# Regrouping the sample rows' narrow matmuls and splitting the opening of the channel mixer in a two-layer decoder step

## The chip, the cores and the metric

The kernel runs on one core of a Trainium2 chip. The metric is device time in microseconds of one execution. Before the change it takes 2732.52 us (median of 3 runs, 2725.46 to 2732.99).

## The reference

Two layers work on 1024 prompt rows and 32 sample rows (8 sequences of 4 new tokens, each with 1024 cached keys in pages), width 1024. Cut to what the change touches:

```python
for l in range(2):
    # sample rows: score all 1028 keys with 8 small index heads, take the best 256, attend
    dots = einsum('bqhd,bsd->bqhs', qi, ki_all) * 64 ** -0.5
    sc   = einsum('bqhs,bqh->bqs', relu(dots), wi)
    _, idx = top_k(where(causal, sc, -inf), 256)
    o = softmax(q @ kg.T * 64 ** -0.5) @ vg          # on the 256 keys taken
    x = layer_norm(ALPHA * x + concat(conv_mixer, o, chunk_mixer) @ w_o)
    h = causal_dwconv3(x @ w_up)                      # 1024 -> 2 x 2816
    x = layer_norm(ALPHA * x + (silu(g) * u) @ w_down)   # g, u = halves of h
```

All inputs and outputs are float32.

## The kernel before

**Stages of a layer.** The input projection with the index, the threshold search, the key and value work, the attention of eight prompt blocks with the sample attention beside blocks 2 to 4, the output projection and norm, then the channel mixer in two parts: 22 chunks of the up projection (`up_chunk`), and the down projection in three teams of 4, 3 and 3 groups (L1919). Large products run as three float32r matmuls (high by high, high by low, low by high), so each operand is split into two parts: ScalarE makes the high part, VectorE or GpSimd subtracts to get the low part (`split`, L618).

**Order.** Every instruction is recorded first (`record`, L317) with a cost from a small model (`cost`, L371) and a priority, which is the program order plus a shift, less a multiple of the length of work behind it. `flush` (L409) then simulates the engines: on each engine the ready instruction of lowest priority goes next, and instructions are issued in that simulated order. Engines take them in that order on the chip. Writers of one PSUM tile on TensorE follow each other in program order (`pe_last`).

**Narrow matmuls.** Three stages of the sample rows use products with 64 or 32 output rows, each put in another part of the same PSUM tile. They are float32 and appear as two records each.
- `index_sample` (L982): per layer 2 x 2 times, two gathered cache tiles (p2 = 0, 1) are transposed, copied to `kgT`, and each half multiplied into 64 rows of one PSUM tile (L1027).
- `scores` (L1346): per layer 8 rounds; four cache tiles are transposed, copied in two copies of two tiles to `kt`, and four products into 32 rows each follow (L1366). `values` (L1405) multiplies, for 8 chunks of keys, four gathered value tiles into 32 rows each.
- `down_sample` (L1874): for each of 10 groups two weight tiles (i = 0, 1), each loaded by a DMA, are multiplied in two halves of columns into 32 rows each of the tile `sm`. The weight tiles lie in the buffers raw, hiA, loA, hiB, loB. The loop over a team's groups is at L1925.

**Opening of the channel mixer.** The up projection is a 2 x 2 block product with seven products, A11.B11, A12.B21, S2.T2, S1.T1, S4.B22, S3.T3, A22.T4, in this order, each 24 matmuls of 128 rows by 268 or 270 columns (`up_product`, L1705). A and S are weights or sums of weights, made by `up_weights` (L1667); B and T are transposed activations or sums of them. `fill` (L1812) makes the activations once per layer, within chunk 0 and ahead of its first product: norms of tiles 6 and 7 (`CARRY`), then for each of the nine tiles a spill to memory, transposes, copies and splits (`put_block`, L1781). Tiles 0 to 3 give B11 and B21; tile t from 4 to 7, with tile t - 4, gives B22, T1 to T4, whose sums GpSimd or VectorE makes. When tile 3 is done, `put_edges` (L1796) writes the first columns of all seven operands.

```python
for t in CARRY:
    layer_norm_direct(fd, y[t], 128, *rows_, D)
for t in (8, 3, 4, 0, 1, 5, 2, 6, 7):
```

Of the kernel before, what the change touches and what calls it, by code (L numbers as in the profile page):

```python
# [19 lines left out]
D = 1024  # L20
# [24 lines left out]
X_OPS = ("B11", "B21", "T2", "T1", "B22", "T3", "T4")  # L45
BIG = float(2.0 ** 100)
MINI, MAXI = -2147483648, 0x7FFFFFFF
NEG = -3.0e38
# [155 lines left out]
class Schedule:  # L204
# [4 lines left out]
    def __init__(self, tc):  # L209
        self.tc, self.nc = tc, tc.nc  # L210
        self.ops = []
        self.hist = {}
        self.free = {e: 0.0 for e in self.LAT}
        self.dma_free = 0.0
        self.base = 0
        self.shift = 0
        self.slack = 0.0
        self.crit = 0.0
        self.tags = {}
        self.slot_of = {}  # L220
        self.fin = {}
        self.held = {}
        self.gone = set()
        self.dead = set()
        self.also = ()
        self.slot_no = {}
        self.stacks = {}
        self.side_of = {}
        self.extents = {}
        self.pe_last = {}  # L230

    def engine(self, name, real):
# [84 lines left out]
    def record(self, eng, fn, method, args, kwargs):  # L317
# [14 lines left out]
        op["slack"] = self.slack  # L332
        op["cost"], op["xfer"] = self.cost(eng, method, kwargs, aps_w, aps_r)
        for write, aps in ((False, aps_r), (True, aps_w)):
            for a in aps:
# [73 lines left out]
    def flush(self):  # L409
# [80 lines left out]
        while done < n:  # L490
# [22 lines left out]
            o = ops[i]  # L513
            o["start"] = start
            end = start + o["cost"]
            self.free[e] = end
# [29 lines left out]
def trunk(ctx: ExitStack, tc: tile.TileContext, A):  # L546
# [293 lines left out]
    for l in range(DEPTH):  # L840
# [141 lines left out]
        def index_sample():  # L982
# [16 lines left out]
            for j in range(2):  # L999
# [17 lines left out]
                for q in range(2):  # L1017
                    kgi = T(wk, [128, 8, 2, 64], F32, "kgi", 1)
                    kT_ = T(wk, [128, 8, 128], F32, "kgT", 1)
                    for p2, kg in enumerate(kgs):  # L1020
# [5 lines left out]
                        ACT.activation(kT_[:, 4 * p2:4 * p2 + 4, :], tp2, AF.Copy)  # L1026
                    for p2 in range(2):  # L1027
                        PE.matmul(dsp[q][64 * p2:64 * p2 + 64], qbd[:, 2 * j + p2, :], kT_[:, 4 * p2:4 * p2 + 4, :],
# [312 lines left out]
        def attend_sample(ts):  # L1341
# [4 lines left out]
            def scores(j):  # L1346
# [10 lines left out]
                for h in range(4):  # L1357
                    kt = T(ts, [128, 4, 2, 128], F32, "kt", KTB)
                    for i in range(2):
# [5 lines left out]
                        copy(kt[:, 2 * i:2 * i + 2], tp2, KT_DVE[(2 * h + i) % len(KT_DVE)])  # L1365
                    for b4 in range(4):  # L1366
                        PE.matmul(ss[h // 2][32 * b4:32 * b4 + 32, 256 * (h % 2):256 * (h % 2) + 256],
# [37 lines left out]
            def values(j):  # L1405
# [6 lines left out]
                for c in range(8):  # L1412
                    for b4, vg in enumerate(vgs):
                        PE.matmul(O[32 * b4:32 * b4 + 32], PT[:, c, 32 * b4:32 * b4 + 32], vg[:, c, :],
# [251 lines left out]

        def up_weights(c):  # L1667
            raws = [T(wp, [128, 1024], F32, "raw", RAWB) if c % 2 == 0 else stride_tile(4 + i)[:, :1024] for i in range(2)]
# [7 lines left out]

            w = slots(("A11", "A12", "S2", "S1"))
            split(*w["A11"], a11)
            split(*w["A12"], a12)
            if c == 0:  # L1680
                w.update(slots(("S4", "S3", "A22")))
# [17 lines left out]
            if c:  # L1699
                split(*w["A22"], a22)  # L1700
            return w

# [26 lines left out]

        def up_chunk(c, between=None):  # L1730
            w = up_weights(c)
            ncf = T(fd, [128, 2, 18], F32, "ncf", 2)
            stf = T(fd, [128, 2, 8, 2], F32, "stf", 2)
            SP.dma_start(stf, A["state_ffn"][l, :, 2 * c:2 * c + 2])
            if between is not None:
                between()
            rg, ru, zg, zu = (stride_tile(t).rearrange("p (h n) -> p h n", h=2) for t in (0, 1, 2, 3 + 4 * (c % 2)))
# [3 lines left out]
            for cut, ps in up_product(ga, w, "A12", "B21", True):  # L1741
                V.tensor_add(rg[:, 0, cut], rg[:, 0, cut], ps)
            for cut, ps in up_product(al, w, "S2", "T2", False):
                ACT.activation(rg[:, 1, cut], ps, AF.Copy)
# [50 lines left out]

        def put_edges():  # L1796
            e11, e21, e12, e22 = edge[:, 0, 0:4], edge[:, 0, 4:8], edge[:, 1, 0:4], edge[:, 1, 4:8]
# [4 lines left out]

            for n, e in (("B11", e11), ("B21", e21), ("B22", e22)):
                put(n, e)
            V.tensor_sub(e12, e22, e12)
# [5 lines left out]

        def fill():  # L1812
            PL.memset(edge, 0.0)
            for t in CARRY:
                layer_norm_direct(fd, y[t], 128, *rows_, D)
            for t in (8, 3, 4, 0, 1, 5, 2, 6, 7):
                r0, n = row(t)
# [8 lines left out]
                elif t < 4:  # L1826
# [4 lines left out]
                    if t == 3:  # L1831
                        put_edges()
                if t >= 4 and t < 8:
# [17 lines left out]
        for c in range(NFF):  # L1851
            zu = up_chunk(c, None if c else fill)
            if c % 2:
# [20 lines left out]
        def down_sample(ps, xs_, raws, begun, last):  # L1874
            for i, x_ in enumerate(xs_):
                for h in range(2):
                    q = 32 * (2 * i + h)
                    PE.matmul(ps[q:q + 32], x_, raws[i][:, 512 * h:512 * h + 512], start=q not in begun,
                              stop=last, skip_group_check=True)
# [39 lines left out]
        for team in TEAMS:  # L1919
# [4 lines left out]
            raws = {g: down_raws(g) for g in gs}  # L1924
            for g in gs:  # L1925
                down_sample(smp, [xf[:, 2 * g + i] for i in range(2)], raws[g], begun, g == NPAIR - 2)
            sch.shift = 0
# [193 lines left out]
```

## Time and profile before

| | |
|---|---|
| median of 3 runs | 2732.52 us |
| profiled execution, its own time | 2729.01 us |
| its span, first to last instruction | 2727.1 us |
| mean granted TensorE clock | 0.979 |
| bytes read from and written to HBM | 193.95 and 64.04 MB |

Busy time is the time in which an engine had at least one instruction running. In a list of instructions the first two numbers are start and duration in microseconds, x is how many were merged in a row, and a bracket shows the idle time before and what ended it. Matmuls are pipelined, so they last longer than the distance to the next. All instructions carry the line 540, at which the planner issues them; they are told apart by their tiles. PSUM tiles of several uses share the name w, and operands of the mixer lie in buffers named a and q.

### The profile page before, as it was taken

How to read it: one execution, taken by the hardware profiler on the slowest of the kernel's cores; microseconds unless marked ns; L12 is line 12 of the kernel's file. 1: busy time of each engine (PE TensorE's matmuls, PEld its weight loads, DVE VectorE, ACT ScalarE, POOL GpSimd, SP SyncE). 2: the span in 40 equal slices, each digit the busy share in tenths (PEclk: the TensorE clock that was granted, in tenths of full speed). 3: DMA queues.
4: the chain of work that ended last, by engine and by line, in shares of the span. 5: the costliest groups of instructions: out<-in, count | busy, mean ns of one | idle time of the engine just before them, and what ended most of it. 6: DMA issues, size and time to landing. Idle time of an engine off the chain costs nothing.

```text
span 2727.1 us, 47611 instructions
## 1 busy us (share of the span) xinstructions
PE 2574.7 (94%) x17217; PEld 2301.5 (84%) x17220; DVE 2179.5 (80%) x4788; ACT 1427.4 (52%) x2796; POOL 1062.6 (39%) x1399
## 2 busy tenths in 40 slices
PE   8989989997999999999999999889889999999996
PEld 7889976787999999777887898668789999997775
DVE  6788888878778777877778988878778777788776
ACT  3678537655444444434446775475544444544433
POOL 5244164563222222543362423635632222225433
PEclk9999999998999999999999999999989999999998
DMA  5021123302223222643231212131123322236432
GB/s 168 17 70 60 55 86 117 103 34 70 95 92 104 98 87 95 241 166 110 79 100 32 65 62 93 60 120 60 56 64 103 102 92 95 87 116 220 167 107 81
DMA packets 120339, 261.07 MB, mean 96 GB/s; under 512 B 29224, under 2 KB 39144, under 8 KB 120104
## 3 DMA queue, kind: packets, MB, share of 16 engines
q1 hardware_dynamic: 114216, 237.07, 26.4%
q0 software_dynamic: 5888, 20.97, 2.4%
q8 instruction: 135, 2.21, 0.3%
q14 instruction: 100, 0.82, 0.1%
HBM read 193.95 MB, written 64.04 MB: 95 GB/s over the span
## 4 chain that ended last, share of the span: by engine, by line
PE 76%; DVE 14%; POOL 2%; ACT 2%; issue 2%; DMA 2%; SPq 1%; POOLq 0%; DVEq 0%; ACTq 0%
PE w L540 70%; DVE y L540 3%; PE wo L540 3%; DVE loA L540 1%; PE o L540 1%; DVE cand L540 1%; DVE gt L540 1%; DVE P L540 1%; PE sm L540 1%; DVE pl L540 1%; DVE q L540 1%; POOL raw L540 1%; PE ss L540 1%; DVE sc L540 1%; SPq L540 1%
## 5 line engine op out<-in xcount | busy, mean ns | idle before, releaser
L540 PE MATMUL w<-q,hiB 128*128 128x268 f32 (+1 forms) x2112 | 402.8, 289 | 2.9 <-DVE y L540 2.3
L540 PE MATMUL w<-q 128*128 128x512 f32 x1680 | 396.2, 395 | 5.3 <-DVE q L540 5.3
L540 PE MATMUL w<-q,hiA 128*128 128x268 f32 (+1 forms) x2112 | 398.2, 288 | 0.0
L540 PEld LDWEIGHTS w<-q 128*128 128x128 f32 x1680 | 313.6, 188 | 98.6 <-issue 20.1
L540 PEld LDWEIGHTS w<-q,hiB 128*128 128x128 f32 x2112 | 331.7, 189 | 9.0 <-DVE y L540 9.0
L540 PEld LDWEIGHTS w<-q,hiA 128*128 128x128 f32 x2112 | 331.0, 189 | 0.0
L540 ACT ACTIVATE y<-w 128x268 f32<-128x268 f32 (+1 forms) x356 | 140.2, 394 | 354.5 <-PE w L540 345.6
L540 PE MATMUL w<-q,loB 128*128 128x268 f32 (+1 forms) x1056 | 304.4, 288 | 0.0
L540 PE MATMUL w<-q,loA 128*128 128x268 f32 (+1 forms) x1056 | 302.9, 287 | 0.0
L540 DVE SCALAR_TENSOR_TENSOR y<-y,cvf,y 128x1075 f32<-128x1075 f32 (+1 forms) x176 | 236.5, 1344 | 46.8 <-ACT y L540 45.8
L540 DVE TENSOR_TENSOR y<-y,w 128x512 f32<-128x512 f32 (+2 forms) x400 | 201.4, 514 | 71.4 <-PE w L540 68.9
L540 ACT ACTIVATE eq<-sc,cand 128x640 bf16<-128x640 f32 (+2 forms) x192 | 192.6, 1003 | 32.7 <-DVE cand L540 28.8
L540 ACT ACTIVATE q<-a 128x512 fp32r<-128x512 f32 x148 | 90.2, 625 | 220.2 <-PE w L540 160.6
L540 PEld LDWEIGHTS w<-q,loA 128*128 128x128 f32 x1056 | 199.6, 189 | 0.0
L540 PEld LDWEIGHTS w<-q,loB 128*128 128x128 f32 x1056 | 199.2, 189 | 0.0
L540 DVE TENSOR_SCALAR_CACHE_REDUCE gt<-sc,cand 128x384 bf16<-128x384 f32 (+4 forms) x204 | 161.7, 792 | 0.9
L540 POOL COPY ncf<-y 128x16 f32<-128x16 f32 (+1 forms) x176 | 108.7, 625 | 111.2 <-DVE y L540 111.2
L540 DVE TENSOR_TENSOR q<-a,q 128x512 fp32r<-128x512 f32 x148 | 124.1, 851 | 28.3 <-ACT q L540 26.0
L540 PE MATMUL w<-a,hiA 128*128 128x270 f32 (+1 forms) x704 | 135.3, 288 | 0.0
L540 POOL TENSOR_SCALAR P<-P,rc 128x128 f32<-128x128 f32 (+7 forms) x104 | 86.0, 837 | 106.5 <-DVE rc L540 79.5
L540 ACT ACTIVATE ph<-w 128x512 fp32r<-128x512 f32 (+1 forms) x160 | 84.3, 554 | 82.4 <-PE w L540 74.1
L540 ACT ACTIVATE y<-y,cvf 128x1076 f32<-128x1076 f32 x88 | 104.8, 1191 | 38.7 <-DVE y L540 34.6
(423 smaller groups left out, 7295.4 us busy)
## 6 DMA issues: line engine op xcount, KB each, us to landing
fspill<-y SPq DMA_DIRECT2D x148, 256.0 KB
a<-fspill SPq DMA_DIRECT2D x148, 256.0 KB
raw<-w_up SPq DMA_DIRECT2D x44, 512.0 KB
y<-w_up SPq DMA_DIRECT2D x44, 512.0 KB
raw<-w_nat SPq DMA_DIRECT2D x20, 512.0 KB
raw<-w_tr SPq DMA_DIRECT2D x16, 512.0 KB
raw<-w_o SPq DMA_DIRECT2D x16, 512.0 KB
yspill<-y SPq DMA_DIRECT2D x16, 512.0 KB
```

The costliest lines, as they stand in the source:

```text
L540: o["fn"](*o["args"], **o["kwargs"])
```

## The change

It reverses the order within the rounds of the index, the scores, the values and the down samples; runs the down samples' groups of the first team as 1, 0, 3, 2 and those of the others last to first; splits `up_weights` into steps and `fill` into two parts, so that tiles 8, 3, 0, 1, 2 and then the first two products come before the other weights, the norms of tiles 6 and 7 and tiles 4 to 7; and adds 0.1 us to the planner's cost of a TensorE instruction whose shape differs from the one before.

```diff
+SHAPE_COST = 0.1
...
+        if eng == "PE":
+            k, m = int(aps_r[0].shape[0]), int(np.prod([int(v) for v in aps_r[0].shape[1:]]))
+            op["shape"] = tuple(32 if v <= 32 else 64 if v <= 64 and aps_r[1].dtype == F32 else 128 for v in (k, m))
...
+            if e == "PE" and o["shape"] != self.shape:
+                self.shape = o["shape"]
+                o["cost"] += SHAPE_COST
             end = start + o["cost"]
...
-                    for p2 in range(2):
+                    for p2 in (1, 0):
                         PE.matmul(dsp[q][64 * p2:64 * p2 + 64], qbd[:, 2 * j + p2, :], kT_[:, 4 * p2:4 * p2 + 4, :],
...
-                    for b4 in range(4):
+                    for b4 in (3, 2, 1, 0):
                         PE.matmul(ss[h // 2][32 * b4:32 * b4 + 32, 256 * (h % 2):256 * (h % 2) + 256],
...
-                    for b4, vg in enumerate(vgs):
+                    for b4, vg in reversed(list(enumerate(vgs))):
                         PE.matmul(O[32 * b4:32 * b4 + 32], PT[:, c, 32 * b4:32 * b4 + 32], vg[:, c, :],
...
-        def up_weights(c):
+        def up_weights(c, w):
...
-            w = slots(("A11", "A12", "S2", "S1"))
+            w.update(slots(("A11", "A12", "S2", "S1")))
             split(*w["A11"], a11)
             split(*w["A12"], a12)
+            yield
             if c == 0:
...
-            return w
+            yield
...
-        def up_chunk(c, between=None):
-            w = up_weights(c)
+        def up_chunk(c):
+            w = {}
+            begin = up_weights(c, w)
+            next(begin)
+            if c == 0:
+                fill((8, 3, 0, 1, 2))
+            else:
+                next(begin)
...
-            if between is not None:
-                between()
...
             for cut, ps in up_product(ga, w, "A12", "B21", True):
                 V.tensor_add(rg[:, 0, cut], rg[:, 0, cut], ps)
+            if c == 0:
+                next(begin)
+                for u in CARRY:
+                    layer_norm_direct(fd, y[u], 128, *rows_, D)
+                put_edges(False)
+                fill((4, 5, 6, 7))
             for cut, ps in up_product(al, w, "S2", "T2", False):
...
-        def put_edges():
+        def put_edges(first):
...
-            for n, e in (("B11", e11), ("B21", e21), ("B22", e22)):
-                put(n, e)
+            if first:
+                for n, e in (("B11", e11), ("B21", e21)):
+                    put(n, e)
+                return
+            put("B22", e22)
...
-        def fill():
-            PL.memset(edge, 0.0)
-            for t in CARRY:
-                layer_norm_direct(fd, y[t], 128, *rows_, D)
-            for t in (8, 3, 4, 0, 1, 5, 2, 6, 7):
+        PL.memset(edge, 0.0)
+
+        def fill(tiles):
+            for t in tiles:
...
-                        put_edges()
+                        put_edges(True)
...
-            zu = up_chunk(c, None if c else fill)
+            zu = up_chunk(c)
...
-            for i, x_ in enumerate(xs_):
+            for i in (1, 0):
...
-                    PE.matmul(ps[q:q + 32], x_, raws[i][:, 512 * h:512 * h + 512], start=q not in begun,
+                    PE.matmul(ps[q:q + 32], xs_[i], raws[i][:, 512 * h:512 * h + 512], start=q not in begun,
...
-            for g in gs:
-                down_sample(smp, [xf[:, 2 * g + i] for i in range(2)], raws[g], begun, g == NPAIR - 2)
+            for g in (1, 0, 3, 2) if first else gs[::-1]:
+                down_sample(smp, [xf[:, 2 * g + i] for i in range(2)], raws[g], begun, g0 == NPAIR - 1 and g == gs[0])
```

## Rows read from the trace of the kernel before

**Rows 1.** The page: busy time of each engine, and the chain that ended last.
```profile
PE 2574.7 (94%) x17217; PEld 2301.5 (84%) x17220; DVE 2179.5 (80%) x4788; ACT 1427.4 (52%) x2796; POOL 1062.6 (39%) x1399
...
PE 76%; DVE 14%; POOL 2%; ACT 2%; issue 2%; DMA 2%; SPq 1%; POOLq 0%; DVEq 0%; ACTq 0%
```

**Rows 2.** Busy time by stretch: length, engines, granted clock, DMA share, GB/s.
```profile
84.00:137.00 53.00, 53.00 (x350) 42.45 (x349) 42.89 (x95) 34.10 (x77) 13.65 (x29) 1.00 0.08 21
1440.00:1485.00 45.00, 45.00 (x295) 35.04 (x293) 36.45 (x78) 30.02 (x70) 11.57 (x21) 1.00 0.09 24
426.00:481.00 55.00, 50.06 (x399) 36.42 (x400) 43.38 (x131) 43.20 (x98) 19.35 (x23) 1.00 0.35 118
1776.00:1835.00 59.00, 53.90 (x411) 39.60 (x411) 42.66 (x127) 41.05 (x91) 18.08 (x21) 0.93 0.27 89
610.00:641.20 31.20, 15.89 (x106) 12.61 (x105) 29.76 (x55) 17.50 (x40) 15.50 (x12) 0.73 0.20 68
1965.80:1998.40 32.60, 16.33 (x106) 13.88 (x106) 31.16 (x56) 17.25 (x40) 15.24 (x13) 0.69 0.29 98
1107.00:1127.00 20.00, 17.66 (x81) 9.70 (x80) 16.86 (x14) 9.82 (x16) 16.80 (x13) 1.00 0.85 309
```

**Rows 3.** TensorE's timeline: two key products of the index, one chunk-mixer round.
```profile
89.13 1.07 PE L540 MATMUL w<-kgT,qbd 128*64 128x512 f32 x2
90.13 0.41 PE L540 MATMUL w<-kiTs,qall 64*128 64x32 f32 x2
...
1467.25 1.07 PE L540 MATMUL w<-kgT,qbd 128*64 128x512 f32 x2
...
38.82 0.66 PE L540 MATMUL w<-wmT,nat 128*64 128x128 f32 x8
39.41 0.42 PE L540 MATMUL w<-hiA,xlo 128*128 128x328 f32 x1
```

**Rows 4.** The chain in order of time, sample attention: start, us, what.
```profile
464.45 0.56 PE ss L540 x4
...
470.87 0.57 PE ss L540 x8
```

**Rows 5.** TensorE's waits: us in total, times, the longest.
```profile
PE ss L540 <- ACT kt L540: 1.5, 2, 1.3
...
PE sm L540 <- DMA raw<-w_down: 1.0, 1, 1.0
```

**Rows 6.** TensorE's timeline: value rounds of the first layer.
```profile
452.68 1.95 PE L540 MATMUL w<-kg,kt 128*32 128x128 f32 x64
...
488.71 1.06 PE L540 MATMUL w<-kg,kt 128*32 128x128 f32 x26
```

**Rows 7.** The chain in order of time, down projection of the first layer.
```profile
1137.07 1.84 PE sm L540 x12
...
1155.40 0.98 PE sm L540 x4
...
1166.54 6.38 DMA raw<-w_down
...
1181.27 0.99 PE sm L540 x8
```

**Rows 8.** TensorE's timeline: opening of the channel mixer, first layer.
```profile
624.74 1.09 PE L540 MATMUL w<-ident,q 128*128 128x128 f32 x4 [10.58 <-DVE ln_ve L540]
...
641.12 0.49 PE L540 MATMUL w<-a,hiA 128*128 128x268 f32 x2
...
648.94 0.28 PE L540 MATMUL w<-q,hiA 128*128 128x268 f32 x1
```

**Rows 9.** Timelines of ScalarE and VectorE in the same opening.
```profile
629.83 0.29 ACT L540 ACTIVATE q<-edge 128x104 fp32r<-128x104 f32 x1 [11.90 <-DVE edge L540]
...
627.80 1.28 DVE L540 SCALAR_TENSOR_TENSOR y<-y,ln_rs,q 128x1024 f32<-128x1024 f32 x1 [1.08 <-POOL ln_rs L540]
...
647.35 0.68 DVE L540 TENSOR_TENSOR q<-w,q 128x512 fp32r<-128x512 f32 x1
```

More of the change, by code (lines that the diff above doesn't have):

```diff
@@ L230, in __init__ @@
         self.pe_last = {}
+        self.shape = None
     def engine(self, name, real):
```

## The prediction

> **What bounds the kernel now.** I read the page first: TensorE is busy 94% of the span and holds 76% of the chain that ended last; VectorE is 80% busy and holds 14% [rows 1]. So time that goes from TensorE counts wherever TensorE has no gaps, and the busy time by stretch says where that is [rows 2]. The index of the sample rows (84 to 137 us, and 1440 to 1485 in the second layer) has none: 53.00 of 53.00 us. The sample attention (426 to 481, 1776 to 1835) is 91% full. The opening of the channel mixer (610 to 641, 1966 to 1998) is the opposite: TensorE works 15.9 of 31.2 us, VectorE 29.8, so VectorE sets its pace. The opening of the down products (1107 to 1127) lies between: TensorE 17.7 of 20, VectorE 16.9, DMA at 0.85.
>
> Then the timeline, for the narrow products. In all three sample stages a product fills only 32 or 64 of the 128 array columns and its neighbours take the others. One 64-wide key product of the index holds TensorE from 89.13 to 90.13, 1.00 us; there are 8 such, all alone, per layer, and the last of the second layer at 1467.25 is as long [rows 3]. The 64-wide products of the chunk mixer, two in each half, are issued together: four of 128 columns, 512 in all, take 0.59 us (38.82 to 39.41), where one key product of 512 columns takes 1.00 [rows 3]. So halves run side by side. In the scores two products (four records) take 0.56 us, and four products (eight records) 0.57 [rows 4]. In the down samples one half-round (four records) takes 0.98, a whole one (eight) 0.99, and twelve records 1.84 [rows 7]. A half-round that stands alone costs as much as a whole one: that is what the regrouping acts on.
>
> **The change part by part.** The durations are of the profiled execution, 2729.0 us; the median of the three runs lies 3.5 us above it.
>
> *Index rounds.* The second half now leads, so the first, ready long before, can follow at once. 8 lone products per layer become 4 pairs: 8 x 1.00 = **8.0 us** over both layers, all on a TensorE without a gap. From below 5, if some pairs are split. Nothing new waits: the tile of both halves was freed by the second before, too.
>
> *Score rounds.* In each layer 7 of 8 rounds stand as two halves of 0.56 and one as a whole. Regrouped that is 14 x 0.56 = 7.8 us. In the first layer 11 of the 14 halves' records lie on the chain of waits (rows such as the first of [rows 4]); 11/14 of 7.8 is **6.1**. Bounds 3 and 7.8: the stretch has 9% of gaps that a shorter TensorE does not close.
>
> *Value rounds.* The first group's 64 records go in one piece, 1.95 us; the second group's are cut into pieces, the largest 26 [rows 6]. Its pieces have 10, 26, 20, 6 and 2 records, and all four operands had landed after the first four products, so it was the plan's priorities that cut, not an operand. Reversing the operands does not mend that. I take **0.5**; from above 3 (both second groups gathered), below 0.
>
> *Down samples.* From 1127 on TensorE is full. There each layer spends now 12 records (1.84), four lone halves before 1190 (0.98 each), two wholes (0.99), two lone halves late in the second team: 9.7 us. After: a two-round piece of the first team 1.84, and three rounds for each of the other teams, 0.99 + 2 x 0.85 = 2.69 (0.85 is what a further round adds, 1.84 - 0.99); 7.2 in all. That is 2.5 per layer. One wait for a weight load, 1.0 us in the first layer [rows 5], goes with it, since the leader is placed at the last load. Together **6.0**. Ahead of 1127 another 3.9 us per layer of rounds would go, but there they fill a TensorE that waits for operands (VectorE 16.9 of 20 us busy [rows 2]): I count 0, from above 7.8. VectorE and DMA are the cover of these rounds; where the operands came earlier they would count. What is moved is only the matmul order; the loads themselves keep theirs on SP's queue. The GpSimd subtractions that overwrite the raw rows must wait for the gathered rounds, but those of a team come two products, 17 us or more, after its start.
>
> *Mixer opening.* The two products A11.B11 and A12.B21 take 6 us and now may start when tiles 0 to 3 stand. But they already overlap the tail: they start at 641.12, while the third product S2.T2 starts only at 648.94 [rows 8], right after VectorE wrote tile 7's last T2 part, from 647.35 on [rows 9]. That is the true end of the opening. VectorE's own work decides it: from 610.74 to 648.03 it has 37.3 us, of which 0.22, 1.08 and 0.40 us are waits and two operations of 0.60 belong to the next chunk's weights. Without these T2 would stand at 645.1: at best **2.9** us per layer. The same splits (some 0.6 us apart), norms of tiles 6 and 7, edges and weight parts remain, in another order; two adds of 0.4 us that came near the end come earlier. The ScalarE stall of 11.9 us [rows 9] and TensorE's of 10.6 [rows 8] behind the norm are covered by the two products in part, but they are not what ends last. From below: the two weight buffers are freed later (eight splits, 4.9 us, go ahead of the S weights), and GpSimd fills them with tile 5's sums: up to -4 per layer. On SP's queue the convolution state comes after five spills instead of before, and is read only after the fifth product; the spills of tiles 4 to 7 and the second chunk's weights, which take the buffers of tiles 4 and 5, move with these tiles and are wanted a whole chunk, some 40 us, later. I take 1.5 per layer, **3.0**, nearer to the gain because the waits named can be filled by the S weights.
>
> *The planner's 0.1 us per change of shape.* It changes planned times, not the choice among ready instructions, and so every later order. No row prices it. Two plans of the same work stand in the trace, one per layer: the sample attention takes 55 and 59 us with 50 and 54 us of TensorE, the opening 31.2 and 32.6 [rows 2]. I take 0, with 5 us either way.
>
> Sum: 8.0 + 6.1 + 0.5 + 6.0 + 3.0 = 23.6 us. From the profiled time that is 2705.4, from the median 2708.9; I give **2707**. With all upper bounds, 38.4 us, 2691; with the lower ones (5 + 3 + 0 + 4 - 8 = 4) 2728.
>
> **The Trainium skill against the rows.** The rows say that most of a lone round is streaming that others could share. The Trainium skill (TensorEngine Tiling (Array Packing), Key Properties) says that changing the tiling mode drains the array. If only that were saved, the price would be the 0.13 us by which 0.98 exceeds the 0.85 of a following round, some 30 x 0.13 = 4 us in all instead of 20. The whole score round at 0.57 speaks against so small a sum; the Trainium skill says in the same place that tiles work independently, and with that the trace agrees.
>
> **The rivals.**
> *The rounds do not stay together.* The planner picks by priority, and another ready instruction may come between leader and followers, as it does in the second value group [rows 6]. For it: that row. Against: each pair of records within a half stands together in every score round I saw. Then perhaps half of index and scores is saved (7), 2.5 in the down stage, 1.5 in the opening: 11 us, 2720.
> *The opening gets longer.* Weight parts and sums later, and TensorE, idle between bursts, at a granted clock of 0.73 and 0.69 in this stretch [rows 2], starts S2.T2 slow. The opening then costs 4 us more per layer instead of 1.5 less: 11 us off the sum, 2718. For it: VectorE has no slack. Against: no operation is added.
> *The leaders wait (the slower side).* A leader that is planned too early stands at the head of TensorE's queue and holds up everything behind it, where before the first half would have run. The Trainium skill (TensorE: Matmul & The Clock Gate, Part 2) says that matmuls keep program order and only weight loads are pulled ahead; that is this mechanism. Its place is the 32 led pieces (8 index, 16 score, 8 down). The longest such wait in the scores is 1.3 us now [rows 5]; a load of down weights that held TensorE took 6.38 us from issue [rows 7]. At 1.3 us each, 42 us: 2747. It decides from 23.6 / 32 = 0.74 us per piece on. Against: all score rounds together wait 1.5 us for their copies now, in 2 of 32 halves [rows 5], and the second half waited for the same copy.
>
> **How the numbers follow.** Forecast 0.62, rounds apart 0.19, longer opening 0.12, waiting leaders 0.07. The likeliest case alone spans 2698 to 2716. The range, 2691 to 2728, takes in the bounds and the first two rivals and leaves out the third. A measurement of this kernel tells about 0.3%, 8 us, from no change, so faster means under 2724: nearly all of the forecast, four fifths of the two middle cases, 0.86. The rest of those is 0.08, and slower 0.06.
>
> **What would show it.** Index: key products in fours of records, one piece of about 1.0 us, four per layer; TensorE's 8.6 us records unchanged but its stretch 4 us shorter. Scores: eight records in 0.57. Down: pieces of 24 records in about 2.7 us. Opening: A11.B11 near 617, S2.T2 near 647, VectorE still full. I am wrong if half-rounds remain, if waits for kt, kgT or w_down appear before leaders at 0.7 us or more, or if the time between the first transpose of the mixer and S2.T2 falls by more than 3 us or grows.

## The result and the profile after

The changed kernel takes 2698.56 us (median of 4 runs, 2696.43 to 2701.80) where the kernel before takes 2731.53 beside it (4 runs): a ratio of 0.9884, with a 95% interval of 0.9866 to 0.9903. That is 33 us faster; the terms of the prediction add up to 23.6, and 2698.56 lies in its range of 2691 to 2728. The profiled execution of the changed kernel took 2699.59 us with a span of 2697.8; the traces of before and after thus differ by 29.3 us, and it is this difference that the stages below must make up. (The profiled execution lies 2.5 us under the median before, 1.0 above it after.)

The page of the changed kernel, its span and busy times (before: [rows 1]):

```profile
span 2697.8 us, 47587 instructions
...
PE 2543.6 (94%) x17220; PEld 2301.1 (85%) x17220; DVE 2191.6 (81%) x4788; ACT 1426.9 (53%) x2796; POOL 1071.4 (40%) x1399
```

TensorE has the same instructions and is busy 31.1 us less (2574.7 before), while the spans differ by 29.3; its gaps add up to 152.4 us before and 154.2 after. VectorE is busy 12 us more. So over the whole span the time came from TensorE's work getting denser, not from fewer gaps, and TensorE stays busy for 94% of it.

TensorE's timeline of the changed kernel, the narrow products of the first layer in order: index, scores, values, down samples. All instructions now carry line 548.

```profile
86.73 1.08 PE L548 MATMUL w<-kgT,qbd 128*64 128x512 f32 x4
...
426.58 1.08 PE L548 MATMUL ss<-kt,qb 128*32 128x256 f32 x8
...
465.36 0.64 PE L548 MATMUL ss<-kt,qb 128*32 128x256 f32 x8
...
482.05 0.64 PE L548 MATMUL w<-kg,kt 128*32 128x128 f32 x16 [0.16 <-DMA kg<-cache_v,gidx]
...
484.96 1.29 PE L548 MATMUL w<-kg,kt 128*32 128x128 f32 x38
...
1168.20 1.07 PE L548 MATMUL sm<-hiA,y 128*32 128x512 f32 x8
1169.09 1.04 PE L548 MATMUL sm<-raw,y 128*32 128x512 f32 x8
1169.94 1.04 PE L548 MATMUL sm<-loB,y 128*32 128x512 f32 x8
```

A pair of key products (four records) now takes 1.08 us, where one alone took 1.07 [rows 3]. All 16 score rounds stand whole. The first one, at 426.58, takes 1.08 us where the others take 0.64: after gaps (5.24 us busy of the 8 from 412 to 420) TensorE's granted clock fell, and until 430 it worked at the lower of its two levels, 1.2 GHz. The stretches 412 to 420 and 420 to 426 (columns as in [rows 2]):

```profile
412.00:420.00 8.00, 5.24 (x39) 4.20 (x37) 6.87 (x16) 6.43 (x14) 5.08 (x5) 0.98 0.85 276
420.00:426.00 6.00, 4.97 (x19) 4.25 (x20) 1.73 (x7) 4.11 (x12) 1.14 (x2) 0.50 0.61 206
```

Three down rounds end at 1170.98, 2.78 us after they began. The second value group remains in pieces (16, 8, 2 and 38 records in the first layer, 64 before it in one piece), much as in [rows 6].

What TensorE waits for in the changed kernel (us in total, times, the longest), and the longest wait of a value round:

```profile
PE w L548 <- DVE q L548: 31.3, 9, 12.0
...
PE w L548 <- DMA kg<-cache_v,gidx: 1.7, 2, 1.5
...
PE ss L548 <- ACT kt L548: 0.7, 1, 0.7
...
PE sm L548 <- DMA loB<-w_down: 0.3, 1, 0.3
```

```profile
1816.91 0.63 PE L548 MATMUL w<-kg,kt 128*32 128x128 f32 x2 [1.52 <-DMA kg<-cache_v,gidx]
```

The leaders (the products now placed first in their round) of the scores and the down samples wait 0.7 and 0.3 us in all, not 0.74 each. Two leaders of the values wait 1.7 us for gathered rows, one of them 1.52; the kernel before has no such wait. The two longest waits of TensorE, for the operand buffer q, are in the two openings of the mixer.

The lengths of the stages, from the first or last instruction of a kind in each trace, for both layers. The first two columns are the kernel before and after; the others are runs told of below (e1: all rounds regrouped; e9: index, scores and values; e7: down samples alone; e2: opening alone; e3: the change without the planner's cost).

| us, first + second layer | before | after | e1 | e9 | e7 | e2 | e3 |
|---|---|---|---|---|---|---|---|
| start (or last down sample) to the attention's first bias | 420.7 + 448.4 | 412.6 + 451.0 | 411.4 + 452.9 | 412.8 + 447.0 | 415.8 + 452.3 | 417.3 + 445.2 | 412.8 + 451.9 |
| attention, to the mixer's first transpose | 189.3 + 199.9 | 190.6 + 193.4 | 190.4 + 189.9 | 187.2 + 193.1 | 190.7 + 197.7 | 189.6 + 200.4 | 190.1 + 190.2 |
| opening, to the first store of the mixer's output | 56.5 + 57.8 | 52.6 + 54.5 | 56.4 + 56.9 | 56.5 + 57.4 | 57.2 + 57.4 | 53.7 + 53.3 | 52.7 + 52.6 |
| rest of the up, and the down to the sums of its samples | 651.0 + 651.1 | 644.2 + 646.6 | 645.2 + 648.9 | 650.3 + 653.8 | 644.6 + 645.7 | 652.9 + 654.3 | 646.5 + 646.6 |

Read by rows, the changed kernel gained 5.5 us ahead of the attention (8.1 in the first layer, 2.6 lost in the second), 5.2 in the attention, 7.2 in the opening and 11.3 in the up and down: 29.2, and 0.1 behind them. Stages that an edit does not touch differ too, from plan to plan and from one execution to the next: e7, which changes nothing ahead of the attention, reaches it 4.9 us earlier than the kernel before. Single entries are good to that and no better. Two rows separate all traces of this case, for either layer: the last row is 644.2 to 648.9 us in the seven kernels with regrouped down samples and 650.3 to 655.5 in the seven without, and the opening is 52.4 to 54.5 in the five with the change's split opening and 56.2 to 57.8 in the eight with the old one (the one kernel left, e8, has a third order).

Busy time by stretch in the changed kernel, for the stretches of [rows 2], placed at about the same work; the openings are cut at the start of S2.T2: length, engines (TensorE, its weight loads, VectorE, ScalarE, GpSimd), granted clock, DMA share, GB/s.

```profile
82.00:136.00 54.00, 52.74 (x388) 46.22 (x387) 46.14 (x91) 36.44 (x82) 19.43 (x34) 1.00 0.09 23
1424.00:1468.00 44.00, 43.76 (x322) 37.59 (x321) 40.12 (x86) 31.99 (x73) 13.53 (x22) 1.00 0.09 25
420.00:475.00 55.00, 50.23 (x408) 39.48 (x409) 42.98 (x130) 41.64 (x96) 18.83 (x22) 0.91 0.33 106
...
603.20:632.30 29.10, 16.31 (x122) 14.58 (x121) 28.53 (x50) 13.96 (x34) 9.60 (x7) 0.81 0.16 49
...
1094.00:1114.00 20.00, 18.71 (x103) 14.26 (x103) 19.47 (x19) 11.35 (x20) 13.22 (x10) 1.00 0.94 345
```

The index has 388 matmul records in 54 us where it had 350 in 53: denser, still with hardly a gap. The opening keeps VectorE at 28.53 of 29.10 us.

### The profile page after: what moved, and what is told of

Same layout as the page of the kernel before. It is cut to its first block, busy times and chain, and to the rows that moved or that the text cites. A ratio compares the mean times of both kernels' runs of the same rounds, so it can differ in the third digit from the quotient of the medians.

```text
span 2697.8 us, 47587 instructions
## 1 busy us (share of the span) xinstructions
PE 2543.6 (94%) x17220; PEld 2301.1 (85%) x17220; DVE 2191.6 (81%) x4788; ACT 1426.9 (53%) x2796; POOL 1071.4 (40%) x1399
## 5 line engine op out<-in xcount | busy, mean ns | idle before, releaser
L548 PE MATMUL w<-q,hiA 128*128 128x270 f32 (+1 forms) x2112 | 400.4, 288 | 1.2 <-ACT y L548 1.0
L548 ACT ACTIVATE y<-w 128x268 f32<-128x268 f32 (+2 forms) x356 | 139.5, 393 | 338.6 <-PE w L548 334.1
L548 PE MATMUL w<-q,loA 128*128 128x270 f32 (+1 forms) x1056 | 302.7, 287 | 0.0
L548 DVE TENSOR_TENSOR y<-y,w 128x268 f32<-128x268 f32 (+2 forms) x400 | 201.9, 515 | 67.1 <-PE w L548 63.8
L548 POOL COPY y<-y 128x32 f32<-128x32 f32 x44 | 10.5, 238 | 293.5 <-DVE y L548 277.8
```

The costliest lines, as they stand in the source:

```text
L548: o["fn"](*o["args"], **o["kwargs"])
```

## The experiments

Each run is timed in rounds with the kernel before on the same chip.

**All rounds, nothing else (e1).** The edit takes the four places with rounds and leaves the opening and the planner as before:

```diff
-                    for p2 in range(2):
+                    for p2 in (1, 0):
...
-                    for b4 in range(4):
+                    for b4 in (3, 2, 1, 0):
...
-                    for b4, vg in enumerate(vgs):
+                    for b4, vg in reversed(list(enumerate(vgs))):
...
-            for i, x_ in enumerate(xs_):
+            for i in (1, 0):
...
-            for g in gs:
+            for g in (1, 0, 3, 2) if first else gs[::-1]:
```

> The kernel before with the rounds of index, scores, values and down samples regrouped; old opening, no cost for a change of shape. Theory R (whole rounds take the TensorE time of half rounds): 20.6 us by the prediction's terms without the opening, so about 2711 us (2703 to 2718), with eight score records in 0.57 us and no half rounds left, whatever the planner's cost is. Rival P (the new plan that the 0.1 us per change of shape makes carries the gain): without that cost little is left, 2722 to 2732 us.

Measured: 2703.37 us against 2725.84, ratio 0.9909 (0.9895 to 0.9923), 22.5 us faster. Theory R holds, at its fast edge, and Rival P falls: alone, the rounds give two thirds of what the change gives.

**The opening, nothing else (e2).** The edit is the change's, without the rounds and with a cost of 0:

```diff
+                fill((8, 3, 0, 1, 2))
...
+                for u in CARRY:
+                    layer_norm_direct(fd, y[u], 128, *rows_, D)
+                put_edges(False)
+                fill((4, 5, 6, 7))
```

> The kernel before with the split opening of the mixer alone. The prediction's step (VectorE's last T2 part ends the opening): 3 us, about 2728, with S2.T2 some 36 to 37 us after the mixer's first transposes, where it was 38.9. The reading of the trace after (the first cut of S2.T2 needs tiles 4 and 5 alone): 6 to 8 us, about 2724, with S2.T2 some 29 us after them and the second chunk's first product some 3 to 4 us earlier, counted from the same start, than in the kernel before.

Measured: 2720.06 against 2725.84, ratio 0.9979 (0.9970 to 0.9988), 5.8 us faster. The opening stage is 2.8 and 4.5 us shorter (table), and S2.T2 starts 29.3 and 29.1 us after the first transposes, as the second reading had it.

**The change without the planner's cost (e3).**

```diff
-SHAPE_COST = 0.1
+SHAPE_COST = 0.0
```

> The changed kernel with the cost for a change of shape set to 0. Theory R: the cost only moves planned times; 2693 to 2705 us, within 5 us of the changed kernel's 2698.6. Rival P: 2710 us or more.

Measured: 2692.48 against 2725.84, ratio 0.9873 (0.9859 to 0.9888). That is as fast as the change with the cost (0.9866 to 0.9903) or a little faster: the rounds stay whole without it. Theory R holds.

**The planner's cost, nothing else (e4).** The kernel before with the change's four edits to the planner, `SHAPE_COST = 0.1` among them; cut to the one that acts:

```diff
+            if e == "PE" and o["shape"] != self.shape:
+                self.shape = o["shape"]
+                o["cost"] += SHAPE_COST
```

> The kernel before with the planner's 0.1 us for a change of shape alone; half rounds stay as they are. Theory R: within 5 us of the kernel before, 2726 to 2737 us, to either side. Rival P: 2720 us or less.

Measured: 2734.67 against 2725.84, ratio 1.0033 (1.0020 to 1.0045), 8.8 us slower. The first layer's attention takes 198.2 us in place of 189.3. No product is added; only the order differs. Rival P falls; the time lies in Theory R's range, but the distance to the kernel before is more than its 5 us.

**The index alone (e5), the scores and values alone (e6), the down samples alone (e7).** Each takes its own lines of the diff of e1:

```diff
-                    for p2 in range(2):
+                    for p2 in (1, 0):
```

> The kernel before with the index's halves reversed alone (old planner costs). Theory R: each pair of halves in one piece of 1.0 us, 8.0 us less, ratio 0.997 (5 to 9 us), the index stretch 4 us shorter in each layer. Rival K (the search and the waits of VectorE behind the index set the end, TensorE's gain goes into a gap): pairs as said, 0 to 3 us less.

```diff
-                    for b4 in range(4):
+                    for b4 in (3, 2, 1, 0):
...
-                    for b4, vg in enumerate(vgs):
+                    for b4, vg in reversed(list(enumerate(vgs))):
```

> The kernel before with scores and values reversed alone. Theory R: all 16 score rounds whole, 5 to 8 us less, ratio about 0.9975. Rival K (the waits for ScalarE, GpSimd and VectorE in this stretch, 9% of TensorE's time, take the gain): 0 to 3 us less. Rival L (leaders wait): waits for kt above 0.7 us in most rounds and more time than before.

```diff
-            for i, x_ in enumerate(xs_):
+            for i in (1, 0):
...
-            for g in gs:
+            for g in (1, 0, 3, 2) if first else gs[::-1]:
```

> The kernel before with the down samples gathered alone. The prediction's term: 6 us less (2.5 per layer behind the opening of the down products, and one load wait), nothing from the opening itself. The reading of the trace after: 10 to 12 us less, since the opening's rounds were on the path too, with TensorE's first wait for VectorE's q there shorter or earlier.

Measured against 2730.45: e5 2727.72, ratio 0.9988 (0.9974 to 1.0001); e6 2733.34, 1.0008 (0.9998 to 1.0018); e7 2716.86, 0.9956 (0.9941 to 0.9970). The down samples alone give some 12 to 14 us, as the second reading had it; the two others next to nothing (both intervals take in 1), and the three gains added make less than e1's 22.5. For e5 that is Rival K by its size; for e6 none of the three theories fits, since the kernel got no faster and the leaders waited 1.5 us in all.

In e5 the attention begins 11.0 us earlier than before and then takes 195.4 us in place of 189.3; with 1.5 and 1.7 us more in the up and down, 2.9 us are left in the trace. In e6 the score products are all whole rounds, and yet the attention of the first layer takes 199.1. Two groups of TensorE's work in that attention, in e6 and then in e3: busy us, mean ns of one, then the idle time before them.

```profile
L540 PE MATMUL w<-ident,P 128*128 128x128 f32 x264 | 44.1, 288 | 6.8 <-POOL P L540 5.4 <-DVE mx L540 1.4
...
L540 PE MATMUL ss<-kt,qb 128*32 128x256 f32 x64 | 5.6, 422 | 0.1
```

```profile
L548 PE MATMUL w<-ident,P 128*128 128x128 f32 x264 | 42.4, 279 | 3.8 <-POOL P L548 3.6
...
L548 PE MATMUL ss<-kt,qb 128*32 128x256 f32 x64 | 5.6, 422 | 0.2 <-ACT kt L548 0.2
```

The scores cost 5.6 us in both (9.4 in the kernel before). What differs is what stands beside them: in e6 TensorE waits 6.8 us ahead of the transposes of P, the prompt blocks' weights, which GpSimd writes, and in e3 3.8. One wait of 3.9 us for P stands at 493 in e6, and around it the granted clock falls to the lower level. The stretch in e6, columns as in [rows 2]:

```profile
479.30:509.30 30.00, 24.52 (x173) 19.88 (x174) 17.06 (x57) 15.13 (x32) 4.17 (x5) 0.83 0.25 82
```

In the kernel before, the clock is 1.00 all through this layer's attention. So part of what is lost here is idle time and part is slower products next to it.

**Norms of tiles 6 and 7 later (e8).** The change without the cost, with tiles 4 and 5 filled ahead of those norms:

```diff
-                for u in CARRY:
-                    layer_norm_direct(fd, y[u], 128, *rows_, D)
                 put_edges(False)
-                fill((4, 5, 6, 7))
+                fill((4, 5))
+                for u in CARRY:
+                    layer_norm_direct(fd, y[u], 128, *rows_, D)
+                fill((6, 7))
```

> The changed kernel with the cost for a change of shape 0 and the norms of tiles 6 and 7 put after the fill of tiles 4 and 5. If the first cuts of the products need tiles 4 and 5 alone, as the trace after is read, TensorE's wait of 10.7 us behind VectorE in the opening shrinks by several us and the kernel gains 4 to 8 us on the version with cost 0, ratio to the kernel before about 0.985. If VectorE's whole work sets the end (the prediction's step), the order of its work does not matter: within 2 us of the version with cost 0.

Measured: 2696.14 against 2730.45, ratio 0.9869 (0.9849 to 0.9889), the same as e3. TensorE's timeline in e8: the start of S2.T2; and what it waits for from the mixer's first transpose at 598.8 on.

```profile
617.33 0.59 PE L548 MATMUL w<-q,hiA 128*128 128x268 f32 x1
```

```profile
PE w L548 <- DVE q L548: 3.8, 4, 1.4
PE w L548 <- POOL raw L548: 2.8, 2, 1.7
PE w L548 <- DVE raw L548: 2.0, 2, 1.4
```

S2.T2 starts 18.5 us after the first transpose, where e3 has 29.2, and the long wait for q is gone. But the stage is no shorter than before to its first store (56.5 us), and only 0.8 us shorter than in e3 to the first product of chunk 1 (49.9 against 50.7). VectorE has 44.06 us of work in those 49.9, TensorE 40.22. The order within the opening moves the waits about; it hardly moves the end, within 2 us as the second theory said, although VectorE is not full here.

**Index, scores and values together (e9).** The index's line and the two lines of the attention from e1's diff, without the down samples:

```diff
-                    for p2 in range(2):
+                    for p2 in (1, 0):
...
-                    for b4 in range(4):
+                    for b4 in (3, 2, 1, 0):
...
-                    for b4, vg in enumerate(vgs):
+                    for b4, vg in reversed(list(enumerate(vgs))):
```

> The kernel before with the index, score and value rounds regrouped; the down samples, the opening and the planner's cost as before. Theory A (the attention's plan takes the gain away and it does not come back by itself): the index alone and the attention alone gave -3 and +3 us, so together within 3 us of the kernel before, ratio 0.999 to 1.001, with the first layer's attention at 195 us or more. Theory B (index and attention give their gain only together): all rounds were 22 us faster where the down samples alone were 13, so the other 9 come here, ratio about 0.9967, the first layer's attention near 190 and the second's near 190.

Measured: 2707.54 against 2729.05, ratio 0.9915 (0.9899 to 0.9931), 21.5 us faster. Theory A falls; B has the kind of result right, but its 9 us are less than half of it. Two edits that alone change the time by -3 and +3 us give together more than twenty. (The single trace of e9 shows 16.2, 9.3 ahead of the attentions and 8.9 in them; its runs go from 2703.31 to 2712.62.) The busy time of the whole attention, first and second layer, in the kernel before, in e6 and in e9; columns as above:

```profile
420.70:610.00 189.30, 179.81 (x1228) 145.75 (x1227) 153.21 (x420) 121.60 (x252) 105.03 (x91) 1.00 0.26 89
1765.90:1965.80 199.90, 186.94 (x1226) 150.78 (x1227) 155.38 (x420) 118.79 (x247) 106.99 (x92) 0.95 0.24 81
```

```profile
419.30:618.40 199.10, 181.93 (x1229) 149.16 (x1228) 155.29 (x420) 122.53 (x252) 105.70 (x90) 0.97 0.25 85
1774.70:1970.80 196.10, 181.11 (x1228) 150.41 (x1227) 155.77 (x420) 118.52 (x247) 106.98 (x91) 0.95 0.24 82
```

```profile
412.80:600.03 187.23, 175.36 (x1226) 144.97 (x1225) 154.43 (x418) 120.29 (x251) 105.88 (x90) 0.99 0.27 90
1753.80:1946.87 193.07, 178.69 (x1228) 147.03 (x1227) 156.67 (x419) 121.23 (x251) 105.80 (x90) 0.97 0.23 81
```

Both layers together, TensorE is busy 366.75 us before, 363.04 in e6 and 354.05 in e9; it is idle 22.45, 32.16 and 26.25. e6 has 3.7 us less work and 9.7 us more gaps; e9 has 12.7 less work and 3.8 more gaps. Busy time includes what the clock costs: the share of full clock that was not granted, times the length, is 10 us before, 15.8 in e6 and 7.7 in e9, an estimate from the lines above and an upper one, since TensorE was idle in part of it. The difference between e6 and e9, 8 of 15 us, may thus be the clock that falls beside the gaps; no run separates the two. The attention of both layers takes 380.3 us in e9, in e1 and in e3; with the index alone 395.3, with the scores and values alone 395.2, with the cost alone 395.4, and 389.2 before.

It goes the other way too. The down samples, worth 12 us alone, add next to nothing behind the index, scores and values: e1, which has all four, is at 0.9909 and e9 at 0.9915, with overlapping intervals. In the traces e1's last row is 10 us shorter than e9's, as the down samples should make it, and 4.5 us are lost ahead of the attentions.

**The change without the score and value rounds (e10).** e3 with these two lines as before:

```diff
-                    for b4 in (3, 2, 1, 0):
+                    for b4 in range(4):
...
-                    for b4, vg in reversed(list(enumerate(vgs))):
+                    for b4, vg in enumerate(vgs):
```

> The changed kernel without the score and value rounds and without the planner's cost: index, down samples and opening alone. Theory A (regrouped scores and values bring nothing of their own): as fast as the changed kernel without the cost, ratio 0.986 to 0.989, attention 190 and 191 us. Theory B (they bring their TensorE time in the full change): 6 to 10 us slower than that, ratio 0.990 to 0.991, attention 196 us or more in one of the layers.

Measured: 2709.21 against 2729.05, ratio 0.9929 (0.9913 to 0.9946). That is Theory B's kind, and more than its 6 to 10 us: without these two lines about 15 us of e3's gain are gone (0.9929 against 0.9873). The attention takes 194.3 and 199.4 us in place of 190.1 and 190.2. TensorE's scores in the second layer, in e10 and in e3:

```profile
L548 PE MATMUL ss<-kt,qb 128*32 128x256 f32 x64 | 10.5, 406 | 0.6 <-DVE kt L548 0.6
```

```profile
L548 PE MATMUL ss<-kt,qb 128*32 128x256 f32 x64 | 5.6, 422 | 0.0
```

4.9 us of the 9.2 in this layer are the score products themselves, 0.6 a wait; in the first layer 9.8 - 5.6 = 4.2, all that it differs by. So the rounds do save their TensorE time; whether the stage keeps it depends on the rest of the plan.

**A cost of 0.05 us, in the change (e11) and alone (e12).** e12 puts the four edits to the planner into the kernel before, with 0.05.

```diff
-SHAPE_COST = 0.1
+SHAPE_COST = 0.05
```

> The changed kernel with a planner's cost of 0.05 us in place of 0.1. Theory A (the value only draws another plan, and the regrouped rounds do not need it): 0.985 to 0.990 with no order by value. Theory B (the cost works against the plan, as it did alone): between the results at 0 and 0.1, 0.9873 to 0.9884. Theory C (the cost keeps rounds together and 0.05 suffices): below 0.986.

> The kernel before with a planner's cost of 0.05 us and nothing else. Theory A (another plan, drawn at random as to its length): any ratio from 0.998 to 1.004, not tied to the 1.0033 at 0.1. Theory B (the cost is harmful in proportion): about +4.5 us, 1.0016, with the first layer's attention between 189 and 198 us.

Measured against 2729.05: e11 2712.14, ratio 0.9928 (0.9912 to 0.9944); e12 2741.93, ratio 1.0040 (1.0024 to 1.0055). Both came out slower than any theory gave in numbers, A for e12 aside, whose upper end this is. With the cost at 0, 0.05 and 0.1 the change takes 0.9873, 0.9928 and 0.9884 of the time before: no order by the value, and a spread of 15 us from the plan alone. In e11 the attention takes 200.2 and 198.1 us, with whole score rounds (6.0 and 5.7 us) and 3.6 us of waits ahead of the transposes of gathered keys, 5.4 ahead of those of P and 2.4 ahead of those of the sample weights Ps, in the first layer. Its granted clock is 0.96 in either layer, where e3 has 0.97 and 0.98. Alone, the cost is slower at both values.

## Why the prediction was right, and where its steps were not

**The mechanism holds.** A half-round that stands alone costs what a whole one does, in index, scores and down samples. TensorE's busy time for the tile sm of the down samples, first layer, in the kernel before and in e7 (length, TensorE, clock, DMA share, GB/s):

```profile
1100.00:1317.50 217.50, 16.47 (x80) 1.00 0.47 160
1100.00:1308.30 208.30, 9.41 (x80) 1.00 0.48 163
```

The same 80 records take 7.1 us less, and as much less in the second layer. The 16 key products of the index take 4.3 us per layer in the changed kernel and 8.6 before. The Trainium skill (TensorEngine Tiling (Array Packing), Key Properties) says that tiles work independently; the whole rounds agree with that (four records of key products in 1.08 us). The smaller price that a saved drain alone would give, some 4 us in all, is refuted by these lines: 14 us for the down samples alone.

**The sum came nearer than its terms.** By the stages of the table the index was taken 2.5 us and the scores and values 1.4 us too large, the down samples 5.3 and the opening 4.2 too small. That these errors partly cancel is luck.

**Down samples: predicted 6.0, measured 11.3 (e7 alone about 12); the step that failed is "Ahead of 1127 ... I count 0".** The stages of e7 are 6.4 and 5.4 us shorter, the changed kernel's 6.8 and 4.5. The prediction took the stretch from 1107 to 1127, with TensorE at 17.66 of 20 us, as one, and let its waits cover the rounds. Cut at the last store of the up (1114.1), the trace of before shows two stretches of which the first is full:

```profile
1100.00:1114.10 14.10, 14.10 (x97) 10.52 (x95) 10.54 (x17) 9.55 (x17) 5.38 (x9) 1.00 0.90 330
```

All of the 2.3 us that TensorE lacked fall after 1114. The rounds before it stand among the products of the last chunk, on a TensorE without a gap, and count. In e7 the up is 3.0 and 3.7 us shorter from its first to its last store, the down from there on 3.4 and 1.7. So the 3.9 us per layer that were counted 0 came almost whole, and the 6.0 came as 5.1. The upper bound of that term (6.0 + 7.8) held it.

**Opening: predicted 3.0, measured 7.2; the step that failed is "That is the true end of the opening", with VectorE's last T2 part in tile 7.** The prediction's own test was that S2.T2 start at most 3 us earlier after the first transpose; it starts 9.9 us earlier (38.9 before, 29.1 after). TensorE's timeline of the changed kernel there:

```profile
609.34 0.90 PE L548 MATMUL w<-a,hiA 128*128 128x268 f32 x2
...
627.99 1.09 PE L548 MATMUL w<-ident,y 128*128 128x128 f32 x4 [10.67 <-DVE q L548]
...
632.27 0.59 PE L548 MATMUL w<-q,hiA 128*128 128x268 f32 x1
...
653.82 0.41 PE L548 MATMUL w<-a,hiA 128*128 128x268 f32 x2
```

Each product is done in two cuts of columns, and the first cut of T2 (268 columns) needs the edges and tiles 4 and 5 alone. At 632.27 tiles 6 and 7 are still being split, as the timeline goes on with their transposes between the products. In the kernel before, S2.T2 stood at 648.94 because the two first products held TensorE from 641.12 without a gap, not because of tile 7 [rows 8]. The two products, 6.5 us from 609.34 on, now lie in time that TensorE had free, and the end of the stage moves by 3.9 and 3.3 us. VectorE, the bound that the prediction named, is full only up to S2.T2 (28.50 of 29.07 us); from there to chunk 1's first product it is TensorE:

```profile
632.27:653.82 21.55, 21.55 (x169) 21.55 (x169) 19.93 (x33) 12.77 (x23) 9.32 (x9) 0.94 0.25 83
```

That an earlier S2.T2 does not by itself end the stage earlier is shown by e8, where a start 10.7 us earlier ends in 0.8: TensorE then waits in many small pieces behind it. What sets the end there was not settled, with VectorE busy 44.06 and TensorE 40.22 of 49.9 us.

**Scores and values: predicted 6.6, got 5.2, by another way than the one told.** The score records went from 9.4 and 10.4 us of TensorE to 5.6 and 5.1, 9.1 in all, against the 7.8 allowed as the most; the two are not quite the same measure, for busy time counts a lone half to its end (0.63), the prediction to the next product (0.56), and two halves of the second layer ran at the lower clock before. The values' second group did stay in pieces, as said. But the first layer kept nothing (1.3 us longer) and the second 6.5. In the first layer the clock fell: 1.00 before, and 0.50 from 420 to 426 after, and in this layer the transposes of gathered keys take 11.5 us in place of 10.1 and those of P 42.8 in place of 41.7. The prediction discounted by 11/14, for the records that lay on the chain of waits. That is the wrong discount: what decides is the order of the whole stage, with the gaps and the clock that come with it. With whole score rounds in both, the attention of the two layers takes 380.3 us in e3 and 398.3 in e11.

**Index: predicted 8.0, its own part about 5; the step that failed is "all on a TensorE without a gap".** The eight lone products per layer did become four pairs, each as long as one lone product was. Busy time from the first to the last product of the index with the tile kiT, first and second layer, in the kernel before and in e5 (columns as above):

```profile
71.40:155.00 83.60, 78.30 (x497) 64.63 (x495) 65.27 (x123) 55.13 (x120) 23.20 (x43) 0.96 0.10 26
1422.30:1500.50 78.20, 74.29 (x474) 60.64 (x473) 64.54 (x120) 52.49 (x116) 21.68 (x38) 0.98 0.10 28
```

```profile
71.10:150.20 79.10, 73.29 (x497) 63.01 (x496) 63.83 (x122) 54.74 (x119) 24.90 (x43) 0.96 0.10 28
1419.10:1496.60 77.50, 70.52 (x473) 60.62 (x472) 63.82 (x120) 53.21 (x116) 22.15 (x38) 0.93 0.10 28
```

TensorE has 5.0 and 3.8 us less to do, as 4.0 each had been forecast. The first layer's stage gets 4.5 us shorter with it, the second's only 0.7: there the gaps grow from 3.9 to 7.0 us, and the granted clock goes from 0.98 to 0.93. The prediction read the gapless stretch of 45 us in the middle; the stage around it has gaps. The changed kernel, 5.5 us earlier at the attention over both layers, agrees, though 3.5 us of its second layer were lost between the down samples' sums and the first of these products (104.8 us before, 108.3 after); where those go was not settled.

**The planner's cost: counted 0, with 5 either way.** Alone it costs 9 us at 0.1 and 11 to 13 at 0.05, outside that bound. In the full change, against none, 0.1 costs about 3 us (the intervals overlap) and 0.05 about 15. No run showed a gain from it.

**The rivals.** That rounds do not stay together: only the second value group. That the opening gets longer: in neither layer. That leaders wait: 1.0 us in all at the scores and down samples and 1.7 at the values, where the prediction had not looked; in e1 single leaders of the down samples wait 1.5 and 0.9 us for their weights, above the 0.7 named as a sign, but they do not add up to the 23.6 that would decide. What none of the rivals named is the interaction: that two of the rounds' edits, each sound, may each be worth nothing until the other is there. What in the planner's choices sends the attention into one class or the other stays open; the waits ahead of P and the gathered keys and the lower clock beside them show where it is paid, not why it is chosen.

**The best version** seen is the change without the cost: e3 with 2692.48 us, 33 us less than the kernel before beside it, and e8, which does not differ from it (0.9869 and 0.9873).

## What to carry to other kernels

Where narrow products share the array, place the one whose operand lands last first in program order: where nothing else is planned between them, the others follow without a gap, and a whole round costs what a half did. Before a stretch's gaps are counted as cover, cut the stretch where they begin; a mean of 88% was a full part (7.1 of 7.1 us) and a waiting part (10.56 of 12.9). With an order made by a planner, what an edit saves can be read from the busy time of its own products, but its effect on the span is only known together with the other edits: time combinations, not only parts.

## What was not expected of the hardware

VectorE and GpSimd slow each other where both read float32 operands from on-chip memory (SBUF). VectorE's timeline in the opening of the changed kernel, and below it GpSimd's:

```profile
617.07 0.69 DVE L548 TENSOR_TENSOR loB<-raw,hiB 128x512 fp32r<-128x512 f32 x1
...
618.34 1.30 DVE L548 TENSOR_TENSOR loA<-raw,hiA 128x512 fp32r<-128x512 f32 x1
...
621.42 2.20 DVE L548 SCALAR_TENSOR_TENSOR y<-y,ln_rs,q 128x1024 f32<-128x1024 f32 x1
...
627.77 1.27 DVE L548 SCALAR_TENSOR_TENSOR y<-y,ln_rs,q 128x1024 f32<-128x1024 f32 x1
...
636.76 2.06 DVE L548 TENSOR_TENSOR q<-w,q 128x512 fp32r<-128x512 f32 x3 [0.23 <-ACT q L548]
```

```profile
617.83 1.26 POOL L548 TENSOR_TENSOR raw<-y,y 128x512 f32<-128x512 f32 x1 [13.99 <-DVE loB L548]
...
621.28 1.26 POOL L548 TENSOR_TENSOR raw<-y,raw 128x512 f32<-128x512 f32 x1
622.50 2.24 POOL L548 TENSOR_TENSOR raw<-y 128x512 f32<-128x512 f32 x1
```

The same split takes 0.69 us with GpSimd idle and 1.30 beside its sum; the same norm step takes 1.27 and 2.20. GpSimd's sums are not all slowed: the one at 621.28, which began before VectorE's norm step, takes 1.26, the one at 622.50, which began during it, 2.24. In these records the one that begins later ends a little less than its own time after the other has ended: 618.34 began beside the sum that ended at 619.09 and ended 0.55 later, 621.42 beside the one that ended at 622.54 and ended 1.08 later, 622.50 beside the norm step that ended at 623.62 and ended 1.12 later. The splits that read the PSUM tile w are not slowed: three from 636.76 on take 2.06 us, 0.69 each, beside GpSimd's sums. GpSimd's records are rough, VectorE's are not: in a stage that VectorE bounds, sums given to GpSimd are not free.
